# Second layer of a hybrid transformer on one core: the mLSTM's queries and keys, its gate chain and the norm before the FFN, issued in another order

## The chip, the cores and the metric

The kernel runs on one core of one Trainium2 chip. The metric is the device time of one execution in microseconds (us), given as the median of three runs. A core has a matrix engine (TensorE, PE in the profile), a vector engine (VectorE, DVE), a scalar engine (ScalarE, ACT), GpSimd (POOL) and SyncE (SP), which here only issues transfers. Each engine takes its own instructions in order, and waits for another engine by semaphores.

## The reference

Two layers of a backbone that carries 256 latent tokens and 256 context tokens of width 1024, all in float32. Cut to what matters here:

```python
for l in range(2):
    sh1, sc1, g1, sh2, sc2, g2 = split(silu(c) @ w_mod[l] + b_mod[l], 6)     # and the same for the context
    h  = rmsnorm(x,  g_pre_mix[l]) * (1 + sc1) + sh1                         # latent; hc is the context's
    u  = h @ w_in[l]                                                         # inputs of four branches
    ya = MLA attention of u[0:3], keys and values from context and latent, rotary dims rotated
    yb = sigmoid(u_o) * (mLSTM forward + mLSTM backward)   # q, k = silu(conv3(u_q, u_k)); log gates cumulated
    yc = windowed attention with a sink, latent keys within 128 positions, all context keys
    yd = real part of a 2-D DFT over positions and channels
    y  = sum_s sigmoid(h @ w_gate[s] + b_gate[s]) * (y_s @ w_branch[s]) @ w_out
    x  = x + g1 * rmsnorm(y, g_post_mix[l])
    h2 = rmsnorm(x, g_pre_ffn[l]) * (1 + sc2) + sh2
    x  = x + g2 * rmsnorm((silu(conv3(a) + b) * v) @ w_down, g_post_ffn[l])  # a, v = h2 @ w_up
```

The first layer does all this for context and latent, the second gives only the latent stream, and the context there serves as keys, values and mLSTM state. Each of the six parts of the modulation (shift, scale, gate, twice) is called a sixth below.

## The kernel before, in words

Activations lie feature-major: 128 features on the partitions, the T = 512 tokens (context first, then latent) along the free axis. A float32 product is made of three matmuls on rounded halves: each operand is split into a high half in the matrix engine's rounded format (`fp32r`) and a low half, the difference, and `mm3_steps` issues high by high (L234), high by low (L235) and low by high (L236) for each of the eight 128-wide pieces of the inner dimension. In the first layer a matmul has 512 columns, in the second, which needs the latent tokens alone, mostly 256. Weights come as tiles of 128 x 1024 by SyncE's DMA queue. ScalarE copies the high half (`parts`, L214, tile `wh`), VectorE subtracts it from the staged tile for the low half (L215, tile `wl`). There are three buffers of each, so a few weights are prepared ahead.

**Order.** TensorE runs in the order in which the code issues. A stage that would leave TensorE waiting is interleaved with *fillers*: generators whose steps are each one group of three matmuls. `fill(us)` draws steps from the head of the list until their columns make up the given microseconds; a debt is carried over. `finish(f)` draws until the generator f is used up. The fillers of a layer are, in order, the mLSTM's queries and keys (`mlstm_qk`, four tiles), the merge of branch 3, the two output-gate tiles (`mlstm_og`), the merge of branch 0 and, after the mLSTM, the window attention's queries and keys and the merges of branches 1 and 2. A merge handles eight tiles; each has a gate product of eight steps, a tanh, and a branch product of two steps. For the other engines a planner orders the instructions by its own costs. Two things override it: SyncE's order within `channel` is the code's, and within a block `in_order()` VectorE's order is the code's too.

**Modulation.** `mod_rounds` computes the sixths from weights that are loaded in 512 KB pieces, a piece a step. There are two forms. In TensorE's, each step is four float32 products (L651, a product of 256 columns by 32). In VectorE's, each step scales the piece and adds it to an accumulator of 128 x 1024, once for each conditioning vector that is needed (L638, L640), and after the eighth piece one set of 16 records on TensorE (L646) sums over the partitions. Either ends with a transpose on VectorE (L654). The steps stand in a queue from which `between()` takes one, once per merge tile and in a few other places, and they are also used as fillers. In the first layer sixths 2, 3 and 4 run there, sixth 3 in VectorE's form.

**The stages that are touched.** In a layer `mixer` issues the token-major products, then `mla`, `mlstm`, `window` and the merges. `mla` computes keys and values, starts the filler `mlstm_qk`, computes the Fourier branch (`fnet`), then four query tiles with their rotation (`rope`, four VectorE operations each), and then `attend`: for each 128 queries and head the scores, their maximum on VectorE, the exponential on ScalarE, a scaling on VectorE (L839), the transposes on TensorE (L845), and the products with the values. Between these stand fillings of 1.2 us, and the first one has 2 us more (`lead`). After it `finish(qk)` draws what is left of the queries and keys. `mlstm` begins with `mlstm_gates`: the forget gate's logarithm (exponential, then logarithm, on ScalarE at L1025 and L1026), its cumulative sums by small matmuls, four transposes into a row of 8 x 512 (copied at L1059), running maxima by scans (L1065 to L1067), the way back to columns, and the row maxima split into three rounded parts (L1079 to L1083). `decays` spreads these rows with a matmul (L1155) and takes exponentials; `scores` multiplies them in (L1194); both run head by head with fillings between.

Before the FFN, `post_end` closes the norm after the merge: it computes the reciprocal root, spreads it over the partitions (`unfold`, L455, tile `rs`) and updates the first two tiles of x. Then `modulate_steps` makes, for each of eight tiles, the product with the spread root (L403), the high half on ScalarE (L406), a copy in full precision on VectorE or ScalarE (L408, L410) and the low half on VectorE (L412). In the second layer the whole runs inside `in_order()`, the first two tiles with their copy on VectorE.

Of the kernel before, what the change touches and what calls it, by code (L numbers as in the profile page):

```python
# [10 lines left out]
F32 = mybir.dt.float32  # L11
F32R = mybir.dt.float32r
BF16 = mybir.dt.bfloat16
I32 = mybir.dt.int32
AF = mybir.ActivationFunctionType
# [140 lines left out]
class Net:  # L156
# [240 lines left out]
    def modulate_steps(self, h, m, segs, r, Am, Bm, vector=False):  # L397

        nc = self.nc
        oc = self.span(segs)  # L400
        hi, lo = h[m]
        t = self.t2([T])
        nc.vector.tensor_tensor(t[:, oc], self.xcols(m, oc), r[:, oc], op=ALU.mult)  # L403
        for cs, b in segs:
            a, s = Am[:, m, b:b + 1], Bm[:, m, b:b + 1]
            nc.scalar.activation(hi[:, cs], t[:, cs], AF.Identity, scale=a, bias=s)  # L406
            if vector:
                nc.vector.tensor_scalar(t[:, cs], t[:, cs], a, s, op0=ALU.mult, op1=ALU.add)  # L408
            else:
                nc.scalar.activation(t[:, cs], t[:, cs], AF.Identity, scale=a, bias=s)  # L410
        yield
        nc.vector.tensor_tensor(lo[:, oc], t[:, oc], hi.bitcast(F32)[:, oc], op=ALU.subtract)  # L412
# [483 lines left out]
    def mla(self, l, h, c0):  # L896
# [48 lines left out]
        wq = self.weights(self.A["wuq"][l], 1024)  # L945
        yf = next(fourier)
        self.fillers.append(self.merge(l, 3, h, yf, c0, True))
        Q = [self.u([2, T]) for _ in range(2)]
        for hd in range(4):
# [13 lines left out]
                    lambda j, i: V[:, j, i], MLA_SCALE, y, room, 2)  # L963
        self.finish(qk)
# [53 lines left out]
    def mlstm_gates(self, l):  # L1018
# [41 lines left out]
        self.fill(4)  # L1060
        MM = self.u([2, T])
        M = [MM[0:8, d] for d in range(2)]
        scan = nc.vector.tensor_tensor_scan
        scan(M[0], br, br, 0.0, op0=ALU.max, op1=ALU.max)
        scan(M[1][:, :CTX][:, ::-1], br[:, :CTX][:, ::-1], br[:, :CTX][:, ::-1], 0.0, op0=ALU.max, op1=ALU.max)  # L1065
        scan(M[1][:, CTX:][:, ::-1], br[:, CTX:][:, ::-1], br[:, CTX:][:, ::-1], M[1][:, 0:1], op0=ALU.max, op1=ALU.max)
        pm = self.pa([2, NT, 8])  # L1067
# [7 lines left out]
        P = self.u([2, T], F32R)  # L1075
        nc.gpsimd.memset(P.bitcast(F32), 0.0)
        for d in range(2):
            t, lo = self.t2([T])[0:8], self.t2([T], F32R)[0:8]
            nc.scalar.copy(P[0:8, d], M[d])  # L1079
            nc.vector.tensor_tensor(t, M[d], P.bitcast(F32)[0:8, d], op=ALU.subtract)  # L1080
            nc.scalar.copy(lo, t)
            nc.scalar.copy(P[32:40, d], t)
            nc.vector.tensor_tensor(P[64:72, d], t, lo.bitcast(F32), op=ALU.subtract)  # L1083
# [42 lines left out]
    def mlstm(self, l, h, c0):  # L1126
# [3 lines left out]
        b, M, E = self.mlstm_gates(l)  # L1130
# [97 lines left out]
        self.fill(3)  # L1228
# [209 lines left out]
    def run(self):  # L1438
# [30 lines left out]
        mod, load = self.mod_rounds(0, (2, 3, 4), nc.gpsimd, (3,))  # L1469
# [20 lines left out]
    def channel(self, l, al, c0, load):  # L1490
# [11 lines left out]
        for seg in segs:  # L1502
            open_steps = []
            with self.in_order() if last else nullcontext():
                if last:
                    self.post_end([seg], True, [lambda f=f, m=m: f(m, [seg]) for m in range(2) for f in (self.scale, self.add)])
                    self.fill(1.5)
                for m in range(KT):
                    if seg is not segs[-1] and m == 4:
                        self.post_end(segs[1:], True)  # L1510
                    if m >= (2 if last else 4) or not last and seg is segs[-1]:
                        self.residual(m, [seg])
                    open_steps.append(self.modulate_steps(h, m, [seg], self.rx, A, B, last and m < 2))
                    next(open_steps[-1])
                    while len(open_steps) > (1 if last and m < KT - 1 else 0):
                        next(open_steps.pop(0), None)
                    if seg is segs[-1]:
                        self.spill(m, c0, c0)
# [58 lines left out]
```

## Time and profile before

| | |
|---|---|
| median of 3 runs | 1440.87 us (1440.1 to 1443.3) |
| profiled execution, its time | 1441.19 us |
| its span, first to last instruction | 1439.4 us |
| TensorE busy | 96% of the span |
| VectorE busy | 67% |
| ScalarE busy | 46% |
| DMA, mean busy share of 16 engines, by queue | 38.3% (SyncE), 5.4% (GpSimd) |

A busy share counts the time in which an engine works on an instruction, and TensorE's matmuls overlap: one may start before the one ahead has ended. The granted clock (PEclk) is the share of TensorE's full speed that the chip granted in a stretch; 1.00 is 2.4 GHz, 0.50 is 1.2 GHz. Over 40 equal slices of the span TensorE shows 9 tenths or more in all but the first, two with 8 and the last; the granted clock shows 9 tenths or more in all but the first and the last. Rows of a timeline give the start in us, the duration in us, the engine, the source line, the operation, the tile written and the tiles read, and their shapes.

The second layer begins its token-major products at about 930 us, MLA at about 955 with its attention from 988, the gates at 1038, the mLSTM's heads at 1053, the window attention at 1110, the merges and the output projection at 1160, the norm at 1224 and the FFN at 1236.

### The profile page before, as it was taken

The numbers are of one execution on the slowest core, as the hardware profiler recorded it, in microseconds if no ns is written. First come the engines' busy times: TensorE is split into PE (matmuls) and PEld (weight loads), VectorE is DVE, ScalarE is ACT, GpSimd is POOL, SyncE is SP. The second block draws the span as 40 slices with busy tenths as digits, with TensorE's granted clock in tenths as the row PEclk, the third lists the DMA queues.
The fourth block names the chain that finished last, engine by engine and source line by source line (L and its number), as shares of the span: only waits on it lengthen the run. The fifth ranks groups of instructions, "written<-read, shape, count | busy, mean of one in ns | idle before, by whom it ended". The sixth has DMA issues, their size and how long they took to land.

```text
span 1439.4 us, 22198 instructions
## 1 busy us (share of the span) xinstructions
PE 1387.3 (96%) x8657; PEld 1173.1 (81%) x8657; DVE 957.4 (67%) x1955; ACT 663.0 (46%) x1156; POOL 36.4 (3%) x69
## 2 busy tenths in 40 slices
PE   6999999999999999999999999899999999899996
PEld 4977777777778888878888888687989898799996
DVE  5458686646644788742554668958676877766666
ACT  3446444224432655332332336656553666455453
POOL 0000000100000000000000000100000000000000
PEclk8999999999999999999999999999999999999998
DMA  9523233442122634443435432552333467357563
GB/s 361 218 73 101 87 121 102 147 163 87 59 74 88 219 121 173 160 137 113 127 110 178 158 98 84 211 211 93 114 118 118 135 195 242 132 172 224 178 183 94
DMA packets 58825, 208.00 MB, mean 145 GB/s; under 512 B 6624, under 2 KB 8032, under 8 KB 58592
## 3 DMA queue, kind: packets, MB, share of 16 engines
q1 hardware_dynamic: 51200, 179.32, 38.3%
q0 software_dynamic: 7520, 27.27, 5.4%
q8 instruction: 68, 1.11, 0.3%
q14 instruction: 37, 0.30, 0.1%
HBM read 201.31 MB, written 5.24 MB: 144 GB/s over the span
## 4 chain that ended last, share of the span: by engine, by line
PE 55%; DVE 7%; ACT 2%; DMA 1%; issue 1%; DVEq 0%; ACTq 0%
PE pg L234 10%; PE pg L235 10%; PE pg L236 10%; PE pa L236 7%; PE pa L235 7%; PE pa L234 7%; DVE wl L215 1%; ACT wh L214 1%; PE pa L792 1%; PE pa L822 1%; PE pa L438 1%; PE pa L861 1%; DMA st<-wgate 1%; PE pa L845 1%; DMA u<-wmod 0%
## 5 line engine op out<-in xcount | busy, mean ns | idle before, releaser
L215 DVE TENSOR_TENSOR wl<-st,wh 128x1024 fp32r<-128x1024 f32 (+2 forms) x262 | 313.9, 1203 | 210.9 <-ACT wh L214 209.6
L214 ACT CAST wh<-st 128x1024 fp32r<-128x1024 f32 (+2 forms) x262 | 268.6, 1032 | 356.1 <-PE pg L235 203.8
L234 PE MATMUL pg<-hh,wh 128*128 128x512 f32 (+1 forms) x1136 | 402.8, 355 | 0.4 <-DVE tg L1271 0.4
L236 PE MATMUL pg<-hh,wl 128*128 128x512 f32 (+1 forms) x1136 | 384.1, 338 | 1.7 <-DVE wl L215 1.5
L235 PE MATMUL pg<-hl,wh 128*128 128x512 f32 (+1 forms) x1136 | 383.3, 337 | 0.0
L234 PEld LDWEIGHTS pg<-hh,wh 128*128 128x128 f32 x1136 | 215.5, 190 | 30.5 <-issue 5.9
L236 PEld LDWEIGHTS pg<-hh,wl 128*128 128x128 f32 x1136 | 215.1, 189 | 26.3 <-DVE wl L215 2.7
L235 PEld LDWEIGHTS pg<-hl,wh 128*128 128x128 f32 x1136 | 215.6, 190 | 23.1 <-issue 3.1
L234 PE MATMUL pa<-hh,wh 128*128 128x256 f32 (+1 forms) x376 | 126.1, 335 | 1.4 <-ACT hh L290 1.4
L235 PE MATMUL pa<-hl,wh 128*128 128x256 f32 (+1 forms) x376 | 126.2, 336 | 0.3 <-DVE hl L291 0.3
L236 PE MATMUL pa<-hh,wl 128*128 128x256 f32 (+1 forms) x376 | 126.0, 335 | 0.0
L234 PE MATMUL pg<-u,wh 128*128 128x256 f32 (+1 forms) x350 | 120.5, 344 | 0.0
L236 PE MATMUL pg<-u,wl 128*128 128x256 f32 (+1 forms) x350 | 115.6, 330 | 0.0
L235 PE MATMUL pg<-u,wh 128*128 128x256 f32 (+1 forms) x350 | 115.4, 330 | 0.0
L234 PEld LDWEIGHTS pa<-hh,wh 128*128 128x128 f32 x376 | 71.3, 190 | 8.7 <-ACT hh L290 1.6
L235 PEld LDWEIGHTS pa<-hl,wh 128*128 128x128 f32 x376 | 71.4, 190 | 8.1 <-DVE hl L291 1.0
L236 PEld LDWEIGHTS pa<-hh,wl 128*128 128x128 f32 x376 | 71.4, 190 | 7.2
L234 PEld LDWEIGHTS pg<-u,wh 128*128 128x128 f32 x350 | 66.3, 190 | 12.2 <-issue 6.2
L235 PEld LDWEIGHTS pg<-u,wh 128*128 128x128 f32 x350 | 66.4, 190 | 6.7 <-issue 1.0
L236 PEld LDWEIGHTS pg<-u,wl 128*128 128x128 f32 x350 | 66.2, 189 | 6.4
L640 DVE SCALAR_TENSOR_TENSOR u<-u,cs,u 128x1024 f32<-128x1024 f32 x49 | 61.6, 1279 | 1.4 <-DMA u<-wmod 1.4
L833 ACT ACTIVATE pp<-pa,nbias 128x512 f32<-128x512 f32 (+1 forms) x48 | 29.5, 614 | 68.0 <-DVE nbias L831 37.2
(296 smaller groups left out, 2129.6 us busy)
## 6 DMA issues: line engine op xcount, KB each, us to landing
st<-wup SPq DMA_DIRECT2D x88, 512.0 KB, 4.1
u<-wmod SPq DMA_DIRECT2D x64, 512.0 KB, 5.8
st<-wgate SPq DMA_DIRECT2D x64, 512.0 KB, 3.7
u<-wmod POOLq DMA_DIRECT2D x32, 512.0 KB, 5.1
st<-wdn SPq DMA_DIRECT2D x32, 448.0 KB, 3.4
st<-win SPq DMA_DIRECT2D x26, 512.0 KB, 3.6
st<-wbr SPq DMA_DIRECT2D x16, 512.0 KB, 3.7
st<-wout SPq DMA_DIRECT2D x16, 512.0 KB, 4.8
```

The lines of the kernel that those rows point to most:

```text
L214: nc.scalar.copy(hi[:, :cols], st[:, :cols])
L215: nc.vector.tensor_tensor(lo[:, :cols], st[:, :cols], hi.bitcast(F32)[:, :cols], op=ALU.subtract)
L234: mm(out, ah, bh, start=i == 0, stop=False)
L235: mm(out, ah, bl, start=False, stop=False)
L236: mm(out, al, bh, start=False, stop=i == n - 1)
L438: self.nc.tensor.matmul(self.s[i][:, :p.shape[-1]], self.one, p, start=first, stop=not first)
L640: nc.vector.scalar_tensor_tensor(t, st, self.cs[:, k, i:i + 1], t, op0=ALU.mult, op1=ALU.add)
L792: ins = self.nc.tensor.matmul(O[:, j], lhs[i], rhs[i], start=i == 0, stop=i == n - 1)
L822: nc.tensor.matmul(S[:, :n], q, k, start=i == 0, stop=i == len(ops) - 1 and not m)
L833: nc.scalar.activation(P[:, :n], S[:, :n], AF.Exp, bias=nb, scale=scale, accum_out=den)
L845: nc.tensor.transpose(S[:, j * 128:j * 128 + 128], P[:, j * 128:j * 128 + 128], self.ident)
L861: ins = nc.tensor.matmul(O[64 * i:64 * i + 64, f], v_of(j, 2 * f + i), PT[i][:, j * 128:j * 128 + 128], start=j == 0, stop=j == n // 128 - 1)
```

## The change

The diff has five parts. In the first layer sixth 4 of the modulation joins sixth 3 in VectorE's form. In the second layer `finish(qk)` stands ahead of the Fourier branch's end and of MLA's query tiles, and the first filling of the attention is 3 us longer than the others, not 2. In the second layer the whole of `mlstm_gates` runs inside `in_order()`; in both layers the splitting of the row maxima is issued right behind the scans, first for both directions the rounded parts and then the last differences, and in the second layer the filling of 4 us stands behind that splitting, not ahead of the scans. In the second layer the filling ahead of the first decays is 5 us, not 3. In the norm before the second layer's FFN the first two tiles get their high half on VectorE straight from the product, and the full-precision copy on ScalarE into a tile of its own; the filling of 1.5 us stands behind tile 3, not ahead of tile 0.

```diff
--- before.py
+++ after.py
@@ -394,13 +394,21 @@
         for _ in self.modulate_steps(h, m, segs, r, Am, Bm, vector):
             pass
 
-    def modulate_steps(self, h, m, segs, r, Am, Bm, vector=False):
+    def modulate_steps(self, h, m, segs, r, Am, Bm, vector=False, first=False):
 
         nc = self.nc
         oc = self.span(segs)
         hi, lo = h[m]
         t = self.t2([T])
         nc.vector.tensor_tensor(t[:, oc], self.xcols(m, oc), r[:, oc], op=ALU.mult)
+        if first:
+            (cs, b), = segs
+            a, s = Am[:, m, b:b + 1], Bm[:, m, b:b + 1]
+            e = self.t2([T])
+            nc.vector.tensor_scalar(hi[:, cs], t[:, cs], a, s, op0=ALU.mult, op1=ALU.add)
+            nc.scalar.activation(e[:, cs], t[:, cs], AF.Identity, scale=a, bias=s)
+            t = e
+            segs = ()
         for cs, b in segs:
             a, s = Am[:, m, b:b + 1], Bm[:, m, b:b + 1]
             nc.scalar.activation(hi[:, cs], t[:, cs], AF.Identity, scale=a, bias=s)
@@ -943,6 +951,8 @@
             nc.gpsimd.tensor_copy(K[i][0:64, 1], kr[0:64])
         qn = self.normed(l, cq, oc, V_GQA, rq)
         wq = self.weights(self.A["wuq"][l], 1024)
+        if c0 > 0:
+            self.finish(qk)
         yf = next(fourier)
         self.fillers.append(self.merge(l, 3, h, yf, c0, True))
         Q = [self.u([2, T]) for _ in range(2)]
@@ -960,8 +970,9 @@
         y = self.newy()
         room = (1.2, 1.2)
         self.attend(range(c0 // 128, NT), lambda i, q, k: [(Q[i // 2][rs[i % 2], i % 2, q], K[i // 2][rs[i % 2], i % 2, k])],
-                    lambda j, i: V[:, j, i], MLA_SCALE, y, room, 2)
-        self.finish(qk)
+                    lambda j, i: V[:, j, i], MLA_SCALE, y, room, 2 if c0 == 0 else 3)
+        if c0 == 0:
+            self.finish(qk)
         return yf, y
 
     def window_qk(self, l, h, c0):
@@ -1057,13 +1068,27 @@
             nc.tensor.transpose(prow[0:8, tt * 128:tt * 128 + 128], b[:, tt], self.ident)
         br = self.t2([T])[0:8]
         nc.vector.tensor_copy(br, prow[0:8])
-        self.fill(4)
         MM = self.u([2, T])
         M = [MM[0:8, d] for d in range(2)]
         scan = nc.vector.tensor_tensor_scan
+        P = self.u([2, T], F32R)
+        nc.gpsimd.memset(P.bitcast(F32), 0.0)
+        if l < L - 1:
+            self.fill(4)
         scan(M[0], br, br, 0.0, op0=ALU.max, op1=ALU.max)
         scan(M[1][:, :CTX][:, ::-1], br[:, :CTX][:, ::-1], br[:, :CTX][:, ::-1], 0.0, op0=ALU.max, op1=ALU.max)
         scan(M[1][:, CTX:][:, ::-1], br[:, CTX:][:, ::-1], br[:, CTX:][:, ::-1], M[1][:, 0:1], op0=ALU.max, op1=ALU.max)
+        ts = [self.t2([T])[0:8] for _ in range(2)]
+        lo = [self.t2([T], F32R)[0:8] for _ in range(2)]
+        for d in range(2):
+            nc.scalar.copy(P[0:8, d], M[d])
+            nc.vector.tensor_tensor(ts[d], M[d], P.bitcast(F32)[0:8, d], op=ALU.subtract)
+            nc.scalar.copy(lo[d], ts[d])
+            nc.scalar.copy(P[32:40, d], ts[d])
+        for d in range(2):
+            nc.vector.tensor_tensor(P[64:72, d], ts[d], lo[d].bitcast(F32), op=ALU.subtract)
+        if l == L - 1:
+            self.fill(4)
         pm = self.pa([2, NT, 8])
         for d in range(2):
             for tt in range(NT):
@@ -1072,15 +1097,6 @@
         for d in range(2):
             s = slice(4 * d, 4 * d + 4)
             nc.vector.tensor_tensor(m[:, :, s], pm[:, d, :, s], cum[:, :, s], op=ALU.add)
-        P = self.u([2, T], F32R)
-        nc.gpsimd.memset(P.bitcast(F32), 0.0)
-        for d in range(2):
-            t, lo = self.t2([T])[0:8], self.t2([T], F32R)[0:8]
-            nc.scalar.copy(P[0:8, d], M[d])
-            nc.vector.tensor_tensor(t, M[d], P.bitcast(F32)[0:8, d], op=ALU.subtract)
-            nc.scalar.copy(lo, t)
-            nc.scalar.copy(P[32:40, d], t)
-            nc.vector.tensor_tensor(P[64:72, d], t, lo.bitcast(F32), op=ALU.subtract)
         E = sm("gE")
         nc.scalar.activation(E, m, AF.Exp, scale=-1.0)
         return b, P, E
@@ -1127,7 +1143,8 @@
         nc = self.nc
         allc, oc = slice(0, T), slice(c0, T)
         ctx_out = c0 == 0
-        b, M, E = self.mlstm_gates(l)
+        with nullcontext() if ctx_out else self.in_order():
+            b, M, E = self.mlstm_gates(l)
         ytm = self.u([NT, 256])
         q0 = c0 // 128
 
@@ -1225,7 +1242,7 @@
 
         Q, KH, KL = self.mlqk
         room = (4.0, 0.8, 2.0) if ctx_out else (2.0, 0.4, 1.5)
-        self.fill(3)
+        self.fill(3 if ctx_out else 5)
         W = decays(0)
         for hd in range(4):
             self.fill(room[0])
@@ -1466,7 +1483,7 @@
             if q == 0:
                 self.tm_start(h, NT)
         self.start2()
-        mod, load = self.mod_rounds(0, (2, 3, 4), nc.gpsimd, (3,))
+        mod, load = self.mod_rounds(0, (2, 3, 4), nc.gpsimd, (3, 4))
         self.queue = [mod]
         for l in range(L):
             last = l == L - 1
@@ -1504,16 +1521,17 @@
             with self.in_order() if last else nullcontext():
                 if last:
                     self.post_end([seg], True, [lambda f=f, m=m: f(m, [seg]) for m in range(2) for f in (self.scale, self.add)])
-                    self.fill(1.5)
                 for m in range(KT):
                     if seg is not segs[-1] and m == 4:
                         self.post_end(segs[1:], True)
                     if m >= (2 if last else 4) or not last and seg is segs[-1]:
                         self.residual(m, [seg])
-                    open_steps.append(self.modulate_steps(h, m, [seg], self.rx, A, B, last and m < 2))
+                    open_steps.append(self.modulate_steps(h, m, [seg], self.rx, A, B, first=last and m < 2))
                     next(open_steps[-1])
                     while len(open_steps) > (1 if last and m < KT - 1 else 0):
                         next(open_steps.pop(0), None)
+                    if last and m == 3:
+                        self.fill(1.5)
                     if seg is segs[-1]:
                         self.spill(m, c0, c0)
         next(self.ws)
```

## Rows read from the trace of the kernel before

**Rows 1.** The page's part 1: busy time, share and instructions of each engine.
```profile
PE 1387.3 (96%) x8657; PEld 1173.1 (81%) x8657; DVE 957.4 (67%) x1955; ACT 663.0 (46%) x1156; POOL 36.4 (3%) x69
```

**Rows 2.** TensorE's waits: what it waited for; us in total, times, longest us.
```profile
...
PE pg L234 <- ACT hh L406: 3.4, 1, 3.4
PE pa L845 <- DVE pp L839: 2.7, 1, 2.7
PE pa L1155 <- DVE u L1083: 1.8, 1, 1.8
...
```

**Rows 3.** Timeline of the norm before the second layer's FFN; start, duration.
```profile
1231.06 0.45 DVE L455 STREAM_TRANSPOSE rs<-n 128x256 f32<-128x256 f32 x1
...
1231.42 0.41 DVE L654 STREAM_TRANSPOSE kr<-pa 128x256 f32<-128x256 f32 x1
...
1233.05 0.41 DVE L408 TENSOR_SCALAR t<-t,A,mod 128x256 f32<-128x256 f32 x1 [0.58 <-ACT hh L406]
1233.37 0.42 DVE L403 TENSOR_TENSOR t<-u,rs 128x256 f32<-128x256 f32 x1
...
1235.26 0.58 PE L235 MATMUL pg<-hl,u 128*128 128x256 f32 x1 [1.62 <-DVE hl L412]
```

**Rows 4.** Window: PE, PEld, DVE, ACT, POOL busy us; clock, DMA share, GB/s.
```profile
300.00:320.00 20.00, 20.00 (x103) 14.79 (x102) 6.29 (x7) 4.92 (x7) 1.58 (x3) 1.00 0.34 117
```

**Rows 5.** Windows where the second layer's MLA attention starts, same columns.
```profile
980.00:1000.00 20.00, 20.00 (x123) 15.52 (x121) 17.50 (x44) 9.93 (x24) 1.05 (x2) 1.00 0.35 120
...
1004.00:1008.00 4.00, 4.00 (x18) 2.97 (x17) 3.88 (x8) 3.30 (x8) 0.00 (x0) 0.57 0.27 65
```

**Rows 6.** TensorE's timeline: a modulation step among fillers, and VectorE's form's sum.
```profile
317.64 0.39 PE L236 MATMUL pg<-hh,wl 128*128 128x512 f32 x1
317.96 0.64 PE L651 MATMUL pa<-u,cs 128*32 128x256 f32 x8
318.53 0.51 PE L234 MATMUL pg<-u,wh 128*128 128x512 f32 x1
318.87 0.39 PE L235 MATMUL pg<-u,wh 128*128 128x512 f32 x1
...
847.35 1.07 PE L646 MATMUL pa<-u,col 128*32 128x256 f32 x16
```

**Rows 7.** The page's part 5: groups of instructions; busy us, mean ns, idle before.
```profile
L215 DVE TENSOR_TENSOR wl<-st,wh 128x1024 fp32r<-128x1024 f32 (+2 forms) x262 | 313.9, 1203 | 210.9 <-ACT wh L214 209.6
...
L640 DVE SCALAR_TENSOR_TENSOR u<-u,cs,u 128x1024 f32<-128x1024 f32 x49 | 61.6, 1279 | 1.4 <-DMA u<-wmod 1.4
```

**Rows 8.** Timeline of the gates in the second layer.
```profile
1043.66 0.67 DVE L1059 COPY t<-pa 8x512 f32<-8x512 f32 x1
...
1044.31 0.28 PE L234 MATMUL pg<-hh,wh 128*128 128x256 f32 x1
1044.43 0.28 PE L235 MATMUL pg<-hl,wh 128*128 128x256 f32 x1
...
1046.20 0.74 DVE L1066 TENSOR_TENSOR_SCAN u<-t,u 8x256 f32<-8x256 f32 x1
...
1050.47 0.38 ACT L1123 ACTIVATE u<-pg 128x256 f32<-128x256 f32 x1
...
1051.64 0.28 DVE L1124 TENSOR_SCALAR u<-u 128x256 f32<-128x256 f32 x1
```

**Rows 9.** By source line: ns least, median, most; first and last start; shape.
```profile
L1081 ACT CAST t<-t x4: 617/619/620, 206.5 to 1051.7; 8x512 fp32r<-8x512 f32 x4
...
L1083 DVE TENSOR_TENSOR u<-t,t x4: 681/682/682, 207.3 to 1052.5; 8x512 fp32r<-8x512 f32 x4
```

**Rows 10.** VectorE's timeline in the mLSTM's last head: eight scalings.
```profile
1092.71 2.47 DVE L1194 SCALAR_TENSOR_TENSOR u<-pa,u 128x256 f32<-128x256 f32 x8
```

**Rows 11.** ScalarE's timeline: the forget gate's logarithm and its table load.
```profile
939.75 1.28 ACT L1026 ACT_TABLE_LOAD   x1
941.04 0.23 ACT L1026 ACTIVATE ge<-ge 128x32 f32<-128x32 f32 x1
```

## The prediction

> **What bounds the kernel now.** I read the page's part 1 first: TensorE is busy for 1387.3 of 1439.4 us [rows 1]. The time can fall in two ways only: less matmul work where TensorE never waits, or a shorter wait of TensorE. So the second view is the list of what TensorE waited for [rows 2]. The reader is to see that the second layer holds three waits that the change aims at: 2.7 us before a transpose of MLA's attention (L845), 1.8 us before the first decay matmul (L1155), and 3.4 us before the FFN's first matmul, to which a further 1.6 us is added at its second [rows 3]. The third view is the stretches: in 300 to 320 us, the first layer's merge, TensorE is busy throughout and VectorE for 6.3 of 20 us [rows 4]. In 980 to 1000 us, where the second layer's attention starts, VectorE is busy for 17.5 of 20 us [rows 5]: there it is nearly the bound itself.
>
> TensorE takes its instructions in the order of the code, so a wait at its head stops all fillers behind it.
>
> **Part 1: one more modulation sixth on VectorE, first layer.** On TensorE a step of a sixth is four fp32 products (eight records). In the trace the matmul before it starts at 317.64, the next but one filler matmul at 318.87 [rows 6]; two ordinary spacings of 0.23 would have been 0.46, so a step costs 1.23 - 0.46 = 0.77 us. Eight steps: 6.2 us. In their place stand 16 records once, 1.07 us and about 0.1 around them [rows 6]: 5.0 us are saved. VectorE gets 16 operations of about 1.28 us [rows 7], 20.5 us, in a stretch of some 50 us (the merge between the mLSTM and the window attention) where it idles for two thirds of the time [rows 4], so they lie beside TensorE's work. Two accumulators more are held, in buffers that the sixth before has just given back. If the cover were gone, a split half of a weight would come late by one operation, 1.3 us, a few times: the term lies between -5.2 and -2.0 us. I take -5.0.
>
> **Part 2: queries and keys ahead of attention, second layer.** The 2.7 us stall goes. After it the granted clock is 0.57 over 4 us [rows 5]: 3.4 us at the 1.2 GHz level, in which half the work is lost, 1.7 us. So 4.4 us are at stake. By the code's tally 15 filler steps of 512 columns are left where the finishing now stands, 15 x 0.69 = 10.3 us of TensorE. In these VectorE can't start on the four rotations, because the queries are now computed after them: it finds some 8 us of work. Then it owes, before the first softmax maximum, the last key tile's chain (3.5), Fourier (2.0), four rotations (6.8), two weight halves (2.4), the maximum (0.6): 15.3 us, and 1.9 us more until the probabilities are scaled (estimates from the operations' lengths in the stretch of rows 5). TensorE reaches the first transposes after Fourier and queries (3.7), 24 filler steps x 0.354 (8.5), the modulation (1.5) and two score products (0.9): 14.6 us. Late by 15.3 + 1.9 - 14.6 = 2.6, of which 0.2 goes for what VectorE does early: 2.4 us, and I charge half of a clock drop, 0.8. What is saved is 4.4 - 3.2 = 1.2 us. Ends: -4.4 (no stall is left) and +3 (below).
>
> **Part 3: the gate chain in trace order, second layer.** This is the dear part. The chain runs inside a block that fixes VectorE's order, and the fillers called inside the block issue their VectorE operations into the same order. That such a block is strict shows in the norm's: the second tile's product (L403, 1233.37) reads only what was ready at 1231.51, yet it stands behind an operation that waits 0.58 us for ScalarE [rows 3]; and a transpose issued by a filler (L654) stands in code order too.
>
> By the tally the merge of branch 3 now ends exactly with attention, so the fillers in the gates are the two output-gate tiles and then branch 0's first. Their weights' low halves (L215, 1.2 us, [rows 7]) come in order:
>
> First, output-gate tile 1: its half stands behind tile 0's closing operation, which waits for tile 0's last matmul and its tanh. From that matmul's start: 0.28 to its end, tanh 0.38, scaling 0.28 [rows 8], half 1.2, with handovers about 2.2 us. TensorE needs it at the third matmul, 0.35 us on (spacing 0.12, [rows 8]): stall 1.8 us.
>
> Second, branch 0's first tile, in the 4 us filling. Its half is issued behind the whole chain, since the filling now follows the chain: copy and scans from 1043.66 to 1046.94 [rows 8], 3.3 us; then a difference 0.68, a cast 0.62, a second cast of the other direction behind it and a last difference [rows 9], in all 3.2 us with ScalarE's order; tile 1's scaling 0.28; the half 1.2: about 8.0 us after the row transposes' end. TensorE has six steps and two matmuls, 20 x 0.12 = 2.4 less 0.3 of the transposes' drain: 2.1. Stall 5.9 us. Nothing else runs on TensorE then. A stall of that length costs at least the clock drop of rows 5, 1.7 us.
>
> Against that the 1.8 us at L1155 [rows 2] goes, since the chain is done long before, and the filling raised from 3 to 5 us hides nothing. Sum: 1.8 + 5.9 + 1.7 - 1.8 = +7.6 us. Ends: -1.8 (the halves aren't held back, a rival) and +10.
>
> **Later in the mLSTM.** The total of fillers is the same, but 10 us of queries and keys are used up earlier and 2 us more are taken before the decays. By the tally branch 0 ends within the last head's scores; its last filling of 0.4 and the one of 1.5 us are empty. The eight scalings of a head take 2.47 us [rows 10] and started 2.3 us late here, so values wait about 0.9 us: +0.9 (0 to +2). At attention's end one filling of 1.2 us is empty too; the copy is done by then: 0.
>
> **Part 4: the norm's first tiles.** Now VectorE's order is: product, high half, product, high half, low half; ScalarE makes the other copy beside it. The reciprocal is spread at 1231.06 and the filler's transposes (L654) no longer follow. Dependent operations of this size start 0.46 apart, others 0.34: product 1231.53, high half 1231.99, product 1232.33, high half 1232.79, low half 1233.13 to 1233.55. The matmul that started at 1235.26 [rows 3] can start at 1233.6: -1.7 us. The first matmul comes 0.6 us earlier, which is worth nothing by itself. The filler's transposes come after tile 3, where VectorE leads TensorE by over 2 us. Ends -3.8 (the slow level that follows is shorter too) and -0.5.
>
> **The sum.** -5.0 - 1.2 + 7.6 + 0.9 - 1.7 = +0.6 us on the profiled execution's 1441.19 (span 1439.4 and 1.8 around it), which is 0.3 above the median 1440.87. On the median: 1441.5 us, no change that shows. What a measurement of this kernel can tell from no change is 0.2%, 2.9 us.
>
> **The rivals.**
>
> *The weight halves aren't held back* (the order binds only the chain, or they are issued ahead). For it: the filling was set behind the chain, which matters only to VectorE's order. Against it: rows 3. Part 3 is then -1.8, the sum -8.8: 1432.1 us. Chance 0.23.
>
> *Slower: VectorE holds attention back.* All of the queries' and keys' work comes ahead of the rotations, and the planner puts further weight halves (1.2 us each) and the modulation's late loads before the first maximum. For it: 17.5 of 20 us [rows 5], and no rotation can start for 10 us. Against it: the third microsecond of lead, and TensorE has 10 us more fillers. It decides from a stall above 4.4 us in place of the 2.7; with 5.5 and a full clock drop part 2 is +2.8, the sum +4.6: 1445.5 us. Chance 0.19.
>
> *Slower: the gates start late.* In the trace of before the forget gate's exponential and logarithm ran 95 us ahead of the chain, in a gap of ScalarE, with a table load of 1.28 us each [rows 11]. If the fixed order keeps them at the chain's place, the first output-gate weights wait behind two loads, two activations of 0.23 and two short VectorE operations, 3.4 us, and the half, 1.2, less what TensorE can do: +4.4, the sum +5.0, 1445.9 us. Chance 0.08. The Trainium skill (ScalarE: Activation LUTs, What ACT_TABLE_LOAD costs) gives a switch of table sets 2.66 us, load and drain together; by that an estimate of this rival is 2.8 us dearer. The trace does not agree: the activation follows 0.01 us after the load's end [rows 11].
>
> **How the numbers follow.** The forecast has chance 0.50 and its own range is 1437 to 1446. Faster by over 0.2%: nearly all of the first rival and a fifth of the forecast's case, 0.32. Slower by over 0.2%: most of the two slower rivals and a sixth of the forecast's case, 0.31. Within: 0.37. The range goes down to the first rival and up past the slower ones: 1431.5 to 1448.
>
> **What would show each step.** Part 1: no short fp32 products in the first layer's merges of branches 0 and 1, 16 records once, and no new wait of TensorE between 270 and 350 us. Part 2: a wait at L845 of 2 to 3 us at the first head, none at the second. Part 3: in the gates two waits of L236 for `wl`, about 1.8 and 5.9 us, a clock near 0.5 after the second, no wait at L1155. Part 4: the FFN's second matmul 1.7 us nearer to the spread. The forecast is wrong if the second wait of part 3 is under 3 us, or if a wait over 4 us stands in attention.

## The result and the profile after

The changed kernel takes 1457.53 us in the median of four runs (1456.41 to 1460.63), beside 1441.24 us for the kernel before in the same session: a ratio of 1.0116, 95% interval 1.0097 to 1.0134. It is 16 us slower; the forecast was no change. The profiled execution took 1456.41 us, its span is 1454.6 us. Of the run e10 below one execution of twelve took 5876.09 us; its ratio leaves that one out.

The first part of the page of the changed kernel, beside [rows 1]:

```profile
PE 1392.1 (96%) x8609; PEld 1180.6 (81%) x8609; DVE 974.3 (67%) x1971; ACT 662.6 (46%) x1156; POOL 36.5 (3%) x69
```

TensorE has 48 records fewer and is busy for longer: part of its work ran at the lower clock. What it waited for in the changed kernel (us in total, times, longest), beside [rows 2]:

```profile
PE pg L236 <- DVE wl L215: 10.0, 6, 4.7
...
PE pa L234 <- ACT t L783: 4.6, 1, 4.6
...
PE pg L234 <- DVE hh L408: 2.2, 1, 2.2
...
PE pa L812 <- DVE u L1241: 1.5, 1, 1.5
```

The waits of 2.7 us in attention and of 1.8 us at the decay matmul are gone, as the change meant. In their place stand a wait of a weight product's third matmul for a low half (L236 for `wl`), up to 4.7 us, and one of a query tile's first matmul for ScalarE (L783 is a copy out of the Fourier branch), 4.6 us. I place every loss by going through the second layer in windows. Idle time is the window less TensorE's busy time, and clock loss is busy time times one less the granted clock. These are windows of the changed kernel from the Fourier branch to the first scores, and of its gates (columns as in [rows 4]):

```profile
986.00:990.00 4.00, 0.72 (x7) 0.53 (x5) 2.51 (x4) 3.64 (x6) 0.00 (x0) 0.98 0.00 0
990.00:994.00 4.00, 2.71 (x12) 2.71 (x13) 3.56 (x8) 3.18 (x8) 0.00 (x0) 0.50 0.38 98
994.00:998.00 4.00, 4.00 (x26) 4.00 (x24) 3.44 (x10) 3.48 (x9) 1.06 (x2) 0.66 0.09 35
998.00:1002.00 4.00, 1.49 (x22) 0.39 (x25) 3.79 (x13) 0.00 (x0) 0.00 (x0) 1.00 0.75 262
...
1052.00:1056.00 4.00, 3.38 (x16) 3.07 (x17) 2.02 (x5) 0.00 (x0) 0.00 (x0) 0.50 0.43 131
1056.00:1060.00 4.00, 2.64 (x14) 2.43 (x13) 3.27 (x5) 2.15 (x5) 0.00 (x0) 0.73 0.00 0
1060.00:1064.00 4.00, 0.66 (x3) 0.66 (x4) 3.54 (x6) 2.76 (x4) 0.00 (x0) 0.69 0.00 0
1064.00:1068.00 4.00, 4.00 (x24) 3.75 (x23) 1.55 (x2) 0.00 (x0) 0.00 (x0) 0.50 0.80 268
1068.00:1072.00 4.00, 4.00 (x20) 4.00 (x20) 1.66 (x4) 1.65 (x3) 0.00 (x0) 0.53 0.32 129
```

The reader is to see two holes, each followed by a stretch at half clock. The account of the spans' 15.2 us, changed kernel less kernel before:

| stretch | idle and clock loss after | before | difference |
|---|---|---|---|
| part 1, up to the second layer's MLA (the last matmul that both issue at the same place starts at 975.34, before at 979.36) | | | -4.0 |
| MLA to its first heads | 7.1 + 2.7 | 2.7 + 1.7 | +5.4 |
| gates | 2.5 + 4.7 idle, 6.5 clock | 1.8 | +11.9 |
| mLSTM's heads, two waits of 1.5 (L236 at 1096.33, L812 at 1125.31) | 3.0 | 0 | +3.0 |
| norm, first sum to second FFN matmul | 13.6 long | 15.3 long | -1.7 |
| FFN and the end | | | +0.4 |

These sum to 15.0. Every row is read from one profiled execution of each kernel.

**The hole in MLA**, from the timeline of the changed kernel (start, duration, engine; in brackets the wait ahead of it):

```profile
986.33 0.39 PE L781 MATMUL pa<-u,k 128*128 128x127 f32 x2
...
989.61 0.75 DVE L1027 SCALAR_TENSOR_TENSOR t<-pg,cw,t 128x510 f32<-128x510 f32 x1
990.28 1.21 DVE L215 TENSOR_TENSOR wl<-st,wh 128x1024 fp32r<-128x1024 f32 x1
990.46 0.63 ACT L1119 ACTIVATE t<-t 128x512 f32<-128x512 f32 x1 [0.73 <-DVE t L1027]
990.99 0.25 ACT L783 COPY t<-pa 128x129 f32<-128x129 f32 x1
...
991.29 0.58 PE L234 MATMUL pa<-u,wh 128*128 128x256 f32 x1 [4.58 <-ACT t L783]
...
1000.71 0.64 PE L659 MATMUL pa<-u,cs 128*32 128x256 f32 x8 [1.92 <-DMA u<-wmod]
```

The Fourier branch now comes after the queries and keys are used up, so its two fillings find no filler. Its four accumulators are written in one go, by 986.7. The first query tile needs an accumulator too and gets one, by the releaser that the profile names, only after a copy at 990.99, which stands in ScalarE's queue behind the convolution and tanh of the last key tile (L1119). Later a modulation piece is late as well.

**The hole in the gates**, from the same timeline:

```profile
1043.59 1.99 ACT L214 CAST wh<-st 128x1024 fp32r<-128x1024 f32 x2
...
1050.73 0.38 ACT L1139 ACTIVATE u<-pg 128x256 f32<-128x256 f32 x1
1051.14 0.29 DVE L1140 TENSOR_SCALAR u<-u 128x256 f32<-128x256 f32 x1 [4.83 <-ACT u L1139]
1051.35 1.22 DVE L215 TENSOR_TENSOR wl<-st,wh 128x1024 fp32r<-128x1024 f32 x1
...
1052.62 0.58 PE L236 MATMUL pg<-hh,wl 128*128 128x256 f32 x1 [2.52 <-DVE wl L215]
...
1058.44 0.38 ACT L1139 ACTIVATE u<-pg 128x256 f32<-128x256 f32 x1 [1.01 <-PE pg L236]
...
1061.16 0.68 DVE L1089 TENSOR_TENSOR u<-t,t 8x512 fp32r<-8x512 f32 x1 [0.41 <-ACT t L1086]
1061.79 1.05 ACT L214 CAST wh<-st 128x1024 fp32r<-128x1024 f32 x1
1061.86 0.29 DVE L1140 TENSOR_SCALAR u<-u 128x256 f32<-128x256 f32 x1
1062.07 2.35 DVE L215 TENSOR_TENSOR wl<-st,wh 128x1024 fp32r<-128x1024 f32 x2
...
1063.34 0.58 PE L236 MATMUL pg<-hh,wl 128*128 128x256 f32 x1 [4.70 <-DVE wl L215]
```

VectorE stood idle for 4.83 us ahead of L1140 with the next low half behind it, whose high half was copied by 1045.6. The second tile's scaling (L1140) could have started once its tanh (1058.44, 0.38 us) was done, and starts at 1061.86, after the chain's last difference (L1089). That VectorE's queue is strictly first in, first out is a sentence of the Trainium skill (PSUM — Partial Sum Buffer, Engine vs sequencer instructions); the trace agrees, with these two rows.

**Part 1 and the norm.** The first layer's merge in the changed kernel, beside [rows 4], and VectorE and TensorE in the norm, beside [rows 3]:

```profile
300.00:320.00 20.00, 20.00 (x89) 16.42 (x88) 16.64 (x18) 5.85 (x7) 2.12 (x4) 1.00 0.57 180
```

```profile
1247.52 0.45 DVE L463 STREAM_TRANSPOSE rs<-n 128x256 f32<-128x256 f32 x1
1248.00 0.42 DVE L403 TENSOR_TENSOR t<-u,rs 128x256 f32<-128x256 f32 x1
1248.46 0.41 DVE L408 TENSOR_SCALAR hh<-t,A,mod 128x256 fp32r<-128x256 f32 x1
...
1249.57 0.41 DVE L420 TENSOR_TENSOR hl<-t,hh 128x256 fp32r<-128x256 f32 x1
...
1250.04 0.58 PE L235 MATMUL pg<-hl,u 128*128 128x256 f32 x1 [0.73 <-DVE hl L420]
```

VectorE's 20.5 us of accumulation lie beside a TensorE that stays busy, and the FFN's second matmul starts 2.5 us after the root is spread; before it was 4.2.

### The profile page after: what moved, and what is told of

Its sections match the earlier page's. It is cut to its first block, busy times and chain, and to the rows that moved or that the text cites. A ratio compares the mean times of both kernels' runs of the same rounds, so it can differ in the third digit from the quotient of the medians.

```text
span 1454.6 us, 22105 instructions
## 1 busy us (share of the span) xinstructions
PE 1392.1 (96%) x8609; PEld 1180.6 (81%) x8609; DVE 974.3 (67%) x1971; ACT 662.6 (46%) x1156; POOL 36.5 (3%) x69
## 4 chain that ended last, share of the span: by engine, by line
PE 75%; DVE 6%; issue 3%; DMA 2%; ACT 1%; DVEq 0%; POOL 0%; ACTq 0%; POOLq 0%
PE pg L234 16%; PE pg L236 15%; PE pg L235 15%; PE pa L235 7%; PE pa L234 7%; PE pa L236 7%; PE pa L800 2%; PE pa L830 1%; DVE wl L215 1%; PE pa L869 1%; PE pa L853 1%; DMA u<-wmod 1%; PE pa L1198 1%; DMA st<-wgate 1%; DMA st<-wup 1%
## 5 line engine op out<-in xcount | busy, mean ns | idle before, releaser
L236 PE MATMUL pg<-hh,wl 128*128 128x512 f32 (+1 forms) x1136 | 386.5, 340 | 10.1 <-DVE wl L215 10.0
L236 PEld LDWEIGHTS pg<-hh,wl 128*128 128x128 f32 x1136 | 217.4, 191 | 35.7 <-DVE wl L215 12.2
L236 PE MATMUL pa<-hh,wl 128*128 128x256 f32 (+1 forms) x376 | 125.9, 335 | 0.0
L236 PE MATMUL pg<-u,wl 128*128 128x256 f32 (+1 forms) x350 | 115.3, 329 | 0.0
L648 DVE SCALAR_TENSOR_TENSOR u<-u,cs,u 128x1024 f32<-128x1024 f32 x63 | 79.0, 1277 | 2.4 <-DMA u<-wmod 2.2
L236 PEld LDWEIGHTS pa<-hh,wl 128*128 128x128 f32 x376 | 71.4, 190 | 7.1
L236 PEld LDWEIGHTS pg<-u,wl 128*128 128x128 f32 x350 | 66.1, 189 | 6.6
L234 PE MATMUL pa<-u,wh 128*128 128x256 f32 (+1 forms) x175 | 60.3, 345 | 4.6 <-ACT t L783 4.6
```

The lines of the kernel that those rows point to most:

```text
L234: mm(out, ah, bh, start=i == 0, stop=False)
L236: mm(out, al, bh, start=False, stop=i == n - 1)
L648: nc.vector.scalar_tensor_tensor(t, st, self.cs[:, k, i:i + 1], t, op0=ALU.mult, op1=ALU.add)
```

## The experiments

Each time is the median of its runs, and each ratio is to the kernel before on the same chip.

| label | what | us | ratio (95%) |
|---|---|---|---|
| e1_gates_free | changed, gates without the fixed order | 1444.4 | 1.0021 (1.0006 to 1.0036) |
| e2_qk_after | changed, queries and keys behind attention | 1445.63 | 1.0034 (1.0021 to 1.0047) |
| e3_qk_behind_fourier | changed, queries and keys behind Fourier | 1455.07 | 1.0100 (1.0086 to 1.0115) |
| e4_parts_1_4 | before, with parts 1 and 4 | 1435.64 | 0.9966 (0.9954 to 0.9978) |
| e5_split_early | e4 with the gates' new order, not fixed | 1433.53 | 0.9941 (0.9928 to 0.9953) |
| e6_lead5 | e4 with a lead of 5 us | 1441.67 | 0.9995 (0.9982 to 1.0009) |
| e7_no_mod_there | changed, no modulation ahead of the scores | 1456.57 | 1.0103 (1.0087 to 1.0118) |
| e8_fill_ahead | changed, filling ahead of the scans | 1452.58 | 1.0073 (1.0058 to 1.0089) |
| e9_qk_after_queries | changed, queries and keys behind the query tiles | 1453.56 | 1.0090 (1.0075 to 1.0106) |
| e10_best_qk_after_queries | e5, queries and keys behind the query tiles | 1440.33 | 0.9993 (0.9979 to 1.0006) |
| e12_best_fill3 | e5 with 3 us ahead of the decays | 1435.52 | 0.9966 (0.9953 to 0.9979) |

**The fixed order in the gates.**

```diff
-        with nullcontext() if ctx_out else self.in_order():
-            b, M, E = self.mlstm_gates(l)
+        b, M, E = self.mlstm_gates(l)
```

> The changed kernel, but the second layer's gate chain isn't inside the block that fixes VectorE's order (the order in the code, the filling behind the splitting and the filling of 5 us stay). Theory (the fixed order holds back the low halves of the fillers' weights): TensorE's waits of 2.5 and 4.7 us for wl in the gates go, and with them the 6.5 us that the granted clock of about 0.5 cost after them; at most the old wait of 1.8 us for the split of the row maxima is back. 1457.5 - 13.7 = about 1444 us, 1446 with the old wait. Rival (the weights come late by their transfers, or because the fillings now end on tile borders): waits for wl or wh of 4 us or more stay in the gates and the time stays above 1451.

1444.4 us: the block, taken out of the change by itself, cost 13.1 us. TensorE's whole list of waits between 1040 and 1075 us in this run:

```profile
PE pg L234 <- ACT tg L1278: 0.6, 1, 0.6
```

No wait for a low half, none at the decay matmul. The theory holds. The place of the filling inside the block:

```diff
-        if l < L - 1:
-            self.fill(4)
+        self.fill(4)
         scan(M[0], br, br, 0.0, op0=ALU.max, op1=ALU.max)
...
-        if l == L - 1:
-            self.fill(4)
```

> The changed kernel, but the 4 us filling in the second layer's gates stands ahead of the scans again; the block with the fixed order and all else stay. Theory (the second wait for wl, 4.7 us, is the low half standing behind the scans and the splitting): that wait falls under 1 us and the 4 us of clock behind it go; the transposes of the maxima then wait about 1 us for the scans. 1457.5 - 8.7 + 1 = about 1450 us. Rival (the half is late for another reason, its transfer or its high half on ScalarE): the wait stays above 3 us and the time above 1455.

1452.58 us, 4.9 faster than the change, where 7.5 was expected. TensorE's waits between 1045 and 1070 us here:

```profile
PE pg L236 <- DVE wl L215: 4.1, 2, 2.5
PE pa L1092 <- DVE u L1079: 1.5, 1, 1.5
PE pa L1092 <- DVE u L1077: 0.2, 1, 0.2
```

The wait of 4.7 us has become 1.6 (4.1 less the first one's 2.5), and the scans' wait is as expected. So the scans and the splitting ahead of the half made most of that wait; the rest is the scaling that waits for its tanh, as at the first.

**The parts that hold.** The kernel before with `mod_rounds(0, (2, 3, 4), nc.gpsimd, (3, 4))` and the new norm, nothing else:

> The kernel before with two parts of the change alone: sixth 4 of the modulation in VectorE's form in the first layer, and the norm's first two tiles on VectorE with the filling behind tile 3. Theory (these two parts keep what the trace of the changed kernel shows for them, 4.0 us ahead at the second layer's MLA and 1.7 us in the norm): 1441.2 - 5.7 = 1435.5 us, between 1434 and 1437. Rival (the gain of the first layer is lost before the end, for instance to a late transfer): 1439 or more.

1435.64 us, as expected: the two parts add up. Then the gates' new order without the block, and 5 us ahead of the decays:

> Parts 1 and 4 as in the run before that had these alone (1435.6 us), and in the gates only the order in the code: the splitting right behind the scans, the filling of 4 us behind it in the second layer, 5 us ahead of the first decays; no block with a fixed order, queries and keys behind attention as before. Theory (the order was good, the block was dear): the 1.8 us wait of the first decay matmul and the 1.6 us of clock after it go, 1432 us (1431 to 1434). Rival (the planner places these operations by its own costs whatever the code's order, or the longer filling takes steps that the heads need): 1435.5 or more, with the wait still there or a new one in the last head.

1433.53 us, the fastest version, 7.8 us below the kernel before beside it. The wait at the decay matmul is gone; TensorE's list between 1030 and 1060 us has one row:

```profile
PE pg L236 <- DVE wl L215: 0.8, 1, 0.8
```

So the order takes the old wait away, and the block had put larger ones in its place. This version is also the changed kernel with the edits of e1 (above) and e2 (below) together. It is 24.0 us below the change; the two edits alone gave 13.1 and 11.9, in sum 25.0. The block and the queries and keys ahead thus carry the whole loss, and add up to within 1 us. Whether the 5 us are needed:

> The fastest version so far (1433.5 us) with the filling ahead of the first decays at 3 us as before, not 5. Theory (with the splitting early and no fixed order the decays' input is there before the filling begins, so the 2 us more hide nothing): no new wait at the decay matmul, the same time within 1.5 us. Rival (the filling is what hides the splitting): the 1.8 us wait is back, with a clock drop, 1435 or more.

1435.52 us. The old wait isn't back, so the filling isn't what hides the splitting; but 2.0 us is more than the 1.5 expected, and the intervals touch. What 5 us are worth stays open within 2 us. Besides, e12 differs from e4 by the gates' new order alone and takes the same time (1435.64 us). The wait of 1.8 us is gone from its trace, but that the order by itself saves time isn't shown.

**Queries and keys ahead.** First back behind attention:

```diff
-        if c0 > 0:
-            self.finish(qk)
         yf = next(fourier)
...
-                    lambda j, i: V[:, j, i], MLA_SCALE, y, room, 2 if c0 == 0 else 3)
-        if c0 == 0:
-            self.finish(qk)
+                    lambda j, i: V[:, j, i], MLA_SCALE, y, room, 2)
+        self.finish(qk)
```

> The changed kernel, but the queries and keys of the mLSTM are finished behind MLA's attention again, with the lead of 2 us; the gates stay as changed. Theory (the queries and keys ahead leave the Fourier branch without a filler, so its four accumulators fill PSUM and the first query tile waits 4.6 us for ScalarE; then a modulation piece comes 2.5 us late): both waits and the 2.5 us of half clock go, the old wait of 2.7 us at the first transposes with its 1.7 us of clock returns: -5.3, about 1452 us. Rival (the stalls in MLA only pay in advance for what the attention would lack): 1457 or more. In the gates the fillers are others, and the two waits for wl should be there again, 2 to 6 us each.

1445.63 us, 11.9 faster than the change, more than twice the 5.3 expected. In MLA the waits are as expected (one of 2.7 at L853, none at the query tile), but this execution has no clock loss behind the 2.7, where 1.7 was counted. In the gates the two waits for `wl` are there again (4.0 and 2.1 us). The rest lies behind MLA: windows over the gates give 10.6 us of idle and clock in place of 13.7, and the heads' two waits of 1.5 us are gone (waits of 0.9 us in sum stand there for an exponential). Those two waits stand in every trace with the queries and keys ahead (the change, e1, e3, e7 to e10) and not in those of e2, e4, e5 and e12, with them behind attention. The steps that queries and keys used up early are what is lacking there; the lead of attention is 2 us in place of 3 besides. Moving them one stage later:

```diff
-        if c0 > 0:
-            self.finish(qk)
         yf = next(fourier)
+        if c0 > 0:
+            self.finish(qk)
```

> The changed kernel, but the queries and keys are finished one step later: behind the end of the Fourier branch and still ahead of MLA's query tiles, so that the Fourier branch's two fillings have steps to draw. Theory (PSUM is full because the Fourier branch stands without fillers): the 4.6 us wait of the first query tile falls under 1 us, and with it the half clock of 2.5 us: 1457.5 - 4.6 - 2.5 = about 1450 us, less if the modulation piece is in time too. Rival (ScalarE and VectorE are late with the queries' and keys' own work whatever stands between): the wait moves to the query tiles' rotations or to the first scores with 3 us or more, and the time stays within 2 us of 1457.5.

1455.07 us, 2.5 faster, between the two. The wait of 4.6 us is gone, and this took its place, TensorE's whole list between 985 and 1002 us:

```profile
PE pa L659 <- DMA u<-wmod: 2.9, 2, 2.3
PE pa L830 <- DVE u L709: 1.8, 1, 1.8
```

TensorE reaches the modulation and the scores earlier and finds the piece and the rotation (L709) not done. Of the 9.8 us of idle and clock in the change 7.0 stay (4.7 of these waits, 2.3 of clock). A lack of accumulators was the form that the lateness took, and at most a part of its ground.

```diff
-        self.between((2, 3)[c0 > 0])
+        self.between((2, 0)[c0 > 0])
```

> The changed kernel, but in the second layer the three modulation steps ahead of MLA's first scores are left in the queue, which takes them later in the merges. Theory (of the 7.1 us that TensorE stands in MLA, 2.5 are the late modulation pieces by themselves): 1457.5 - 2.5 = 1455 us. Rival (VectorE is late until the fourth rotation at 1002 us whatever TensorE does before): the same 2 to 3 us stand at the first maximum's transposes or at the scores, and the time is within 1 us of 1457.5. In both the 4.6 us wait of the first query tile stays.

1456.57 us, within 1 us of the change, as the rival said; but the executions of either kernel spread over more than the 1.5 us between the two forecasts, so the theory's 1455 isn't excluded. The trace, of an execution of 1465.0 us, the slowest of the five, shows 1.1 us at the scores (L830) and 2.3 us at a filler's low half in place of the 2.5 us for the piece. The waiting moved; that it costs nothing isn't shown. Then with the rotations ahead of the queries and keys:

```diff
-        if c0 > 0:
-            self.finish(qk)
         yf = next(fourier)
...
+        if c0 > 0:
+            self.finish(qk)
         self.fill(1)
         self.between((2, 3)[c0 > 0])
```

> The changed kernel, but the queries and keys are finished behind MLA's four query tiles, still ahead of the first scores, so that VectorE gets the rotations first and TensorE has the queries' and keys' products beside them. Theory (the 9.6 us that TensorE loses ahead of the first scores, 7.1 idle and 2.5 by the clock, come from an order that puts all covering work before the work it should cover): the 4.6 us wait of the first query tile goes, no wait over 1 us stands before the first scores, and the time is 1457.5 - 8 = about 1450 us. Rival (VectorE and ScalarE simply have too much to do before the first maximum, in whatever order): the same 5 us and more stand at the first scores or transposes, and the time is 1455 or more.

1453.56 us: 4.0 faster where the theory said 8 and the rival at most 2.5. The timeline of this run:

```profile
991.34 1.12 PE L830 MATMUL pa<-u,u 96*128 96x512 f32 x2
...
996.91 0.69 DVE L308 TENSOR_TENSOR u<-t,u 64x512 fp32r<-64x512 f32 x1 [0.59 <-ACT u L306]
...
998.42 0.68 DVE L835 TENSOR_REDUCE nm<-pa 128x1 f32<-128x512 f32 x1
...
1000.52 0.39 PE L234 MATMUL pg<-u,wh 128*128 128x256 f32 x1 [3.76 <-ACT tg L1279]
```

The first scores start at 991.34 without a wait, but VectorE takes their maximum at 998.42, behind the last key tile (L308). ScalarE's tanh for a filler (L1279) is queued behind the exponential that needs the maximum, and TensorE loses 3.8 us there and 1.5 by the clock after it. So of the 9.8 us some 4.5 come from the order of TensorE's work (4.0 by the medians), and 5.3 are work that VectorE and ScalarE owe before the first softmax in this order too. On the fastest version:

> The fastest version so far (parts 1 and 4, the splitting early, no fixed order: 1433.5 us), and in the second layer the queries and keys finished behind MLA's query tiles and ahead of the first scores, with the lead of 3 us. Theory: the 2.7 us wait in attention and its 1.5 us of clock go, and the mLSTM, which then lacks these fillers, waits about 3 us as it did in both kernels with queries and keys ahead: 1433.5 - 4.2 + 3 = about 1432 us, no clear gain. Rival (the rotations first don't help): waits of 3 us or more ahead of the first maximum, 1437 or more.

1440.33 us, 6.8 slower than without it: the rival, with the same 3.8 us wait and the two of 1.5 us in the heads. And the other way to fill the old 2.7 us wait:

> Parts 1 and 4 alone (1435.6 us), and the first filling of the second layer's attention is 5 us longer than the others in place of 2; queries and keys stay behind attention. Theory (the 2.7 us wait at the first transposes can be filled with the steps that stand behind the attention, without moving the queries and keys): the wait goes and the clock drop behind it where there was one, 1435.6 - 2.7 = 1433 us, down to 1431. Rival (VectorE is the bound there: the longer filling brings more weight halves to VectorE ahead of the maximum): the wait stays above 1.5 us at this or a later head and the time is within 1 us of 1435.6.

1441.67 us, 6 slower than e4: the wait stays, as the rival said, and the time is worse than it said. The waits of its profiled execution between 985 and 1006 us:

```profile
PE pg L234 <- DVE nbias L837: 3.0, 1, 3.0
PE pg L236 <- DVE wl L215: 0.3, 1, 0.3
```

3.0 us at a filler in place of 2.7 at the transposes, here with 2.8 us of clock loss behind it, where e4's execution has none. That explains why nothing is gained; that execution took 1436.7 us, and why the median is 5 us above it isn't settled.

## Why the prediction was wrong

- Part 1 (-5.0): right. 4.7 us between the mLSTM's first decay matmul (210.5, after 210.8) and the norm's sums (510.5, after 506.1), and 4.0 us at the second layer. Between the two lies the first layer's norm, where after two waits for modulation pieces TensorE lost 1.5 us at the lower clock and stood 0.9 us less than before.
- Part 2 (-1.2): this step failed, in place and in size. I let VectorE be late at the first transposes, "after Fourier and queries (3.7), 24 filler steps x 0.354 (8.5)". The estimate of VectorE's debt was of the right kind (3.2 with clock; e9 shows 5.3). But TensorE stood before it got that far: between the queries' and keys' end and the first scores the code issues only the four filler steps of `fill(1)` (996.6 to 998.1 us), and none ahead of the query tiles. My sum set 24 filler steps against a debt that falls due before most of them. That order costs some 4.5 us more (e9), with the wait of 4.6 us at the first query tile; my sign of failure was a wait of that size, though in attention and not ahead of it. My slower rival had the cause, the queries' and keys' work ahead of the rotations, but not the place; its price for part 2 was +2.8, measured +5.4 in MLA, beyond my upper end of +3 for the part too. By the medians the whole of part 2, with what it takes from the mLSTM, costs more: 11.9 us in the changed kernel (e2), and 10.9 without the block (e1 against e5).
- Part 3 (+7.6): the mechanism and both places were right: 2.5 and 4.7 us for 1.8 and 5.9, together 7.2 for 7.7, and no wait at the decay matmul. The term that was mis-sized is the clock: I took 1.7 us, once; both waits were followed by a slow stretch, 6.5 us in all. Hence 11.9, above my upper end of +10.
- Later in the mLSTM (+0.9): 3.0 us. Neither wait is at the values that I had named. One is for a weight's low half in the heads (L236). The other is at the transposes of the finished rows (L812), whose last scaling by the normalizer (L1241) VectorE reaches behind two low halves, of which this is the second:

```profile
1123.05 1.22 DVE L215 TENSOR_TENSOR wl<-st,wh 128x1024 fp32r<-128x1024 f32 x1
...
1125.31 0.33 PE L812 MATMUL pa<-k,u 128*128 128x128 f32 x1 [1.48 <-DVE u L1241]
```

- Part 4 (-1.7): right, 1.7.
- The rival that the halves aren't held back is refuted by e1 and e8. That the gates start late is too: the logarithm's table load ran at 935.75 us, far ahead of the chain, as in [rows 11].

The sum was wrong by 14.6 us of span (+15.2 for +0.6): 6.6 are part 2, 4.3 part 3 (4.8 its clock, less 0.5 for the waits), 2.1 the heads, 1.0 part 1 and 0.4 the end; 0.2 are not placed.

## What to carry to other kernels

Where one engine's order is fixed and helpers of the streaming engine issue into the same block, list what each waiting instruction of the chain has behind it: here the chain lost nothing without the block, and 13 us with it. Work that is moved ahead as cover has to be tallied at each place that it leaves, since those places need it as cover too. And price each stall with the slow clock that may follow it, as a range: the same short wait had none behind it in one execution and 1.7 us in another (below).

## What the runs showed of the hardware

A wait of 2.5 us in the gates was followed by some 5 us at a granted clock of 0.50 (1052 to about 1058), and one of 4.7 us by about 8 us of it (1064 to 1071.6, where the matmul spacing falls from 0.21 to 0.12 us). The clock thus cost 6.5 us beside 7.2 us of standing.

The same wait isn't followed by the same loss in every execution. The 1.8 us at the decay matmul were followed by windows at 1.00 in the kernel before, and by a loss of 1.7 us in e4. The 2.7 us in attention were followed by a loss of 1.7 us in the kernel before and of 1.5 in e5, and by none in e2, in e4 and in e12 (where 2.4 us are left of the wait). The 2.5 us of waits for modulation pieces between 998 and 1002 us in the changed kernel, broken by short products, were followed by windows at 1.00; 2.8 us of the same waits in e1 were followed by 0.50. The windows behind the 1.8 us (before, then e4) and behind the pieces in e1:

```profile
1052.00:1056.00 4.00, 2.71 (x22) 2.69 (x22) 3.09 (x7) 3.78 (x10) 0.00 (x0) 1.00 0.45 132
1056.00:1060.00 4.00, 4.00 (x23) 2.99 (x22) 4.00 (x12) 4.00 (x15) 0.00 (x0) 1.00 0.72 243
...
1048.00:1050.00 2.00, 1.90 (x11) 1.94 (x12) 1.73 (x3) 1.32 (x5) 0.00 (x0) 0.65 0.09 29
1050.00:1052.00 2.00, 2.00 (x11) 2.00 (x11) 0.90 (x1) 1.98 (x5) 0.00 (x0) 0.50 0.81 221
...
1004.00:1006.00 2.00, 2.00 (x6) 1.04 (x5) 1.87 (x4) 0.00 (x0) 0.00 (x0) 0.50 0.15 16
```

What a wait costs by the clock could here be read only from the stretch behind it, and in that execution alone.
